# Attention stage of a hybrid decoder trunk: casts of weight pieces moved to GpSimd, four result splits made one, query projections taken in five passes

## The chip, the core and the metric

The kernel runs on one core of a Trainium2 chip. The metric is the device time of one execution in microseconds. Before the change it is 1218.23 us, the median of three runs (1217.66 to 1218.72). The five engines of the core are named as in the profile: PE (TensorE, matrix products; PEld is its loading of stationary operands), DVE (VectorE), ACT (ScalarE), POOL (GpSimd) and SP (SyncE, which here only issues DMAs).

## The reference

The input is one sequence of 512 rows with 1024 features in float32. Layer one is a gated recurrence with a SwiGLU feed-forward block. Then keys and values are computed once. Layer two is attention with another SwiGLU block. Only the attention matters here:

```python
def dilated_attention_mixer(h, w_q, q_norm, w_o, k, v, cos, sin):
    q = (h @ w_q).reshape(B, S, N_GROUPS, Q_HEADS, HEAD_DIM)      # 3 groups, 8 heads, 128
    q = apply_partial_rope(rms_norm(q, q_norm[:, None, :]), cos, sin)
    ...
    for g, (window, dilation) in enumerate(DILATION_GROUPS):      # (128,1), (512,4), (2048,16)
        o, l = dilated_window_attention(q[:, :, g], k[:, :, g], v[:, :, g], window, dilation)
    wts = softmax(stack(lses), axis=0)
    o = sum(wts[..., None] * stack(outs), axis=0)
    return o.reshape(B, S, 1024) @ w_o
```

There are two key/value heads, and each serves four query heads.

## The kernel before

**Exact products from two parts.** Every float32 operand of a large product is split into a high part in a shorter format (`fp32r`) and the low part that is left, and `mm3` (lines 146 to 148) or lines 703 to 705 issue three products for one: high by high, high by low, low by high. A weight comes in pieces of 128 x 1024 numbers, 512 KB each.

**The weight stream** is the class `Stream`. A piece `i` is loaded by SP into a tile `wr` (line 85, two buffers). Line 100 casts it to its high part `wh`, always on ACT. The low part `wl` is made in one of two ways. For most pieces DVE subtracts (line 107). For pieces marked "dma", which are the query weights `w_q`, the output weights `w_o` and seven pieces of the first stage, ACT writes minus one times the piece in the short format into `wl` (line 103), and a DMA issued by POOL adds the piece from memory once more onto it (line 104). `wh` and `wl` have three buffers each. `ws.get(i)` hands out piece `i` and prepares pieces up to `i+2` (`ws.asp = 2` in this stage), so the tiles of piece `i` become free when PE is done with piece `i-3`.

**Query projections** (`project_q`, `project`). For one key/value head a pass computes, for one group `g`, four tiles of 128 rows by 512 columns (four heads) from four pieces. A pass over all four row tiles takes 16 steps, four to a piece; one step is six products of 512 columns. A pass over two row tiles takes 8 steps, two to a piece, and loads the four pieces for itself. When a row tile is finished, `collect` scales and squares it, `rotate` applies the rotation, `normed` the factors, and `turn` transposes it on PE (line 781) and copies it out on ACT (line 783, `qt`). `at(n, ...)` holds such follow-up work for n ticks of a counter that each step advances.

**The units.** Attention proper is 32 units: two key/value heads, four row tiles, four phases. A unit has `scores` (PE products with keys, two DVE instructions for mask and minimum, the exponential on ACT at line 854, the reciprocal on DVE, the division on POOL at line 856); three units later `turned` (PE transposes at line 868, high part `ph` on ACT and low part `pl` on DVE by `halve`, lines 228 and 229); four units later, for odd phases, `values`. After the fourth phase of a row tile `values` writes the results of four heads: for the first three row tiles of the first head they are copied to `o_t`, for the other five row tiles they are split at once into `xh` and `xl`, head by head, by four calls of `halve`.

**Filling.** Head 0's projections run before the units. A table `plan` spreads the work for head 1 and the first half of the output projection (`out_half`, generator `o0`) between units: each row of it has a generator, a number of steps and the first and last unit between which they are dealt out. `q1` has 48 steps: a full pass for each of groups 0 and 1, and two half passes for group 2. Its first 11 steps (`START_Q`) run ahead of the units.

**The order on an engine** is fixed when the program is built. The code is recorded as written, a scheduler then places instructions by priority, and splits of weight pieces are recorded with high priority. On the chip each engine runs its list in that order, waiting by semaphores.

Of the kernel before, what the change touches and what calls it, by code (L numbers as in the profile page):

```python
# [69 lines left out]
class Stream:  # L70


    def __init__(self, tc, nc, pool, pieces, ahead_load, ahead_split):
        self.tc, self.nc, self.pool, self.pieces = tc, nc, pool, pieces
        self.al, self.asp = ahead_load, ahead_split
        self.raw, self.parts = {}, {}
        self.nl = self.ns = self.cut = 0
        self.hold = {}

    def _load(self, i):  # L80
# [10 lines left out]
    def _split(self, i):  # L91
        nc = self.nc
        r, w = self.raw.pop(i)
        hi = self.pool.tile([128, 1024], F32R, name=f"wh{i}", tag="wh")
        lo = self.pool.tile([128, 1024], F32R, name=f"wl{i}", tag="wl")
        self.parts[i] = (hi, lo)

        def do(c):
            with self.tc.high_priority():
                nc.scalar.copy(hi[:, c], r[:, c])  # L100
                kind = self.pieces[i][1]
                if kind == "dma":
                    nc.scalar.mul(lo[:, c], r[:, c], -1.0)  # L103
                    nc.gpsimd.dma_start(lo[:, c], self.pieces[i][0][:, c], accum_op=ALU.add)
                else:
                    eng = nc.gpsimd if kind == "pool" else nc.vector
                    a = eng.tensor_tensor(lo[:, c], r[:, c], hi[:, c].bitcast(F32), ALU.subtract)  # L107
# [32 lines left out]
def trunk(tc, A, out):  # L140
# [27 lines left out]

    p_f1 = ffn_pieces("f1_in", "f1_out")
    p_kv = add_pieces([A["w_kv"][i] for i in range(12)])  # L170
    p_q = add_pieces([A["w_q"][i] for i in (*range(24), *range(20, 24))], "dma")
    p_o = add_pieces([A["w_o"][i] for i in range(8)], "dma")
    p_f2 = ffn_pieces("f2_in", "f2_out")

    with tc.tile_pool(name="keep", bufs=1) as kp, tc.tile_pool(name="wts", bufs=3) as wp, \
# [104 lines left out]
        with tc.tile_pool(name="lru", bufs=2) as lp, \  # L280
# [243 lines left out]
STATS = 5  # L524
N_PR = 4
LAG_T, LAG_V = 3, 4
START_Q = 11


def rotary(tc, A, rp, tp):  # L530
# [67 lines left out]
def attention(tc, A, ap, ws, env):  # L598
# [170 lines left out]
    qt = {}  # L769

    def project_q(kv):
        for g in range(3):

            for j, tiles in enumerate((range(2), range(2, 4)) if kv and g == 2 else (range(4),)):
                def done_q(t, ps, g=g, st={}, tiles=tiles):
                    collect(ps, 4, t - tiles[0], len(tiles), st, t, 3 + g)
                    if t == tiles[-1]:
                        def turn(j, rows):
                            pt = bank("PT")
                            for i in range(4):  # L780
                                PE.transpose(pt[:, 128 * i:128 * i + 128], rows[:, 128 * i:128 * i + 128], ident)  # L781
                            q = ap.tile([128, 4, 4, 32], F32, name="qt", bufs=12)
                            S.copy(q, pt.rearrange("q (h p i) -> q p h i", h=4, p=4))
                            qt[j, kv, g] = q
                            if not kv and not j:
                                query_part(0, 0, g)

                        normed(st, 4, 0, turn, 8 if len(tiles) > 2 else 5, tiles)

                yield from project(p_q + 12 * kv + 4 * g + 4 * j, xh, xl, done_q, tiles)  # L790

    def first(fn):

# [81 lines left out]
    def values(kv, n, p):  # L875
# [21 lines left out]
        if kv == 0 and n < 3:  # L897
            S.copy(o_t[:, :, ns].rearrange("q h (p i) -> q h p i", p=4), src)
        else:
            for i in range(4):  # L900
# [136 lines left out]
```

## Time and profile before

| what | value |
|---|---|
| three timed runs, median (range) | 1218.23 us (1217.66 to 1218.72) |
| the profiled execution: its own time; its span | 1220.25 us; 1218.3 us |
| PE busy, share of span | 1204.8 us, 99% |
| DVE, ACT, POOL busy | 658.2, 514.4, 157.2 us |
| DMA, mean | 113 GB/s |
| mean granted clock of PE | 0.998 |

The sum of a prediction is made against the 1220.25 us of the profiled execution; 1.95 us of it lie outside the span. The stages can be told by their lines: recurrence to about 160 us, first feed-forward to about 520 us, keys and values to about 585 us, head 0's query projections and the first steps of head 1's to about 673 us, the units with their filling to about 828 us, then the rest of the output projection and the second feed-forward.

In the groups of the profile a row names line, engine and operation, output and inputs, count, busy time and mean duration, then the idle time of the engine ahead of these instructions and what ended it. In the tables by windows each engine has its busy time in the window and the number of instructions, then the granted clock (1.00 is full), the mean busy share of the 16 DMA engines and their GB/s.

### The profile page before, as it was taken

How to read it: one execution, taken by the hardware profiler on the slowest of the kernel's cores; microseconds unless marked ns; L12 is line 12 of the kernel's file. 1: busy time of each engine (PE TensorE's matmuls, PEld its weight loads, DVE VectorE, ACT ScalarE, POOL GpSimd, SP SyncE). 2: the span in 40 equal slices, each digit the busy share in tenths (PEclk: the TensorE clock that was granted, in tenths of full speed). 3: DMA queues.
4: the chain of work that ended last, by engine and by line, in shares of the span. 5: the costliest groups of instructions: out<-in, count | busy, mean ns of one | idle time of the engine just before them, and what ended most of it. 6: DMA issues, size and time to landing. Idle time of an engine off the chain costs nothing.

```text
span 1218.3 us, 14685 instructions
## 1 busy us (share of the span) xinstructions
PE 1204.8 (99%) x5627; PEld 995.6 (82%) x5627; DVE 658.2 (54%) x1237; ACT 514.4 (42%) x758; POOL 157.2 (13%) x159
## 2 busy tenths in 40 slices
PE   8999999999999999999999999999999999999998
PEld 6778888888888888888888887898888888888887
DVE  7787674454544333377564567765554455542221
ACT  6795433233232222265555667655423232222110
POOL 0100001011110000010411243341011011110000
PEclk9999999999999999999999999999999999999999
DMA  6643333323233333333988666335223323233341
GB/s 237 145 104 104 104 106 104 104 87 103 87 103 100 89 100 96 100 96 94 227 179 178 135 153 151 79 70 137 88 87 104 103 88 104 87 100 112 113 115 44
DMA packets 40757, 137.62 MB, mean 113 GB/s; under 512 B 5104, under 2 KB 5744, under 8 KB 40688
## 3 DMA queue, kind: packets, MB, share of 16 engines
q1 hardware_dynamic: 32976, 112.00, 28.9%
q0 software_dynamic: 6704, 23.60, 11.0%
q10 hardware_dynamic: 1008, 1.09, 0.3%
q8 instruction: 44, 0.72, 0.2%
q14 instruction: 25, 0.20, 0.0%
HBM read 133.53 MB, written 2.10 MB: 111 GB/s over the span
## 4 chain that ended last, share of the span: by engine, by line
PE 94%; DVE 3%; ACT 2%; DMA 1%; issue 0%; SPq 0%; DVEq 0%; ACTq 0%
PE ps L147 25%; PE ps L148 25%; PE ps L146 25%; PE ps L703 5%; PE ps L705 5%; PE ps L704 5%; DMA wr<-in_w_in 1%; PE ps L781 1%; PE ps L868 1%; PE ps L387 1%; PE ps L386 1%; ACT wh L100 0%; DVE sqc L640 0%; PE ps L245 0%; DVE pl L229 0%
## 5 line engine op out<-in xcount | busy, mean ns | idle before, releaser
L100 ACT CAST wh<-wr 128x1024 fp32r<-128x1024 f32 (+3 forms) x212 | 215.4, 1017 | 480.9 <-PE ps L147 444.3
L146 PE MATMUL ps<-xh,wh 128*128 128x512 f32 x896 | 352.7, 394 | 0.6 <-ACT xh L223 0.6
L148 PE MATMUL ps<-xh,wl 128*128 128x512 f32 x896 | 349.5, 390 | 0.4 <-DVE wl L107 0.4
L147 PE MATMUL ps<-xl,wh 128*128 128x512 f32 x896 | 349.4, 390 | 0.1
L107 DVE TENSOR_TENSOR wl<-wr,wh 128x1024 fp32r<-128x1024 f32 (+2 forms) x169 | 240.9, 1426 | 148.3 <-ACT wh L100 148.2
L146 PEld LDWEIGHTS ps<-xh,wh 128*128 128x128 f32 x896 | 168.3, 188 | 37.5 <-ACT xh L223 1.5
L147 PEld LDWEIGHTS ps<-xl,wh 128*128 128x128 f32 x896 | 168.5, 188 | 36.1 <-issue 1.7
L148 PEld LDWEIGHTS ps<-xh,wl 128*128 128x128 f32 x896 | 168.4, 188 | 35.8 <-DVE wl L107 0.8
L146 PE MATMUL ps<-gh,wh 128*128 128x512 f32 x352 | 137.0, 389 | 0.0
L148 PE MATMUL ps<-gh,wl 128*128 128x512 f32 x352 | 136.9, 389 | 0.0
L147 PE MATMUL ps<-gl,wh 128*128 128x512 f32 x352 | 136.9, 389 | 0.0
L491 POOL TENSOR_TENSOR u<-u,g 128x512 f32<-128x512 f32 x44 | 58.8, 1336 | 503.4 <-ACT wh L100 354.2
L490 DVE TENSOR_TENSOR u<-ps,rb 128x512 f32<-128x512 f32 x44 | 30.4, 691 | 135.9 <-PE ps L148 135.9
L703 PE MATMUL ps<-wh,xh 128*128 128x512 f32 x224 | 91.5, 408 | 0.4 <-DVE sqc L640 0.4
L705 PE MATMUL ps<-wh,xl 128*128 128x512 f32 x224 | 88.0, 393 | 0.0
L704 PE MATMUL ps<-wl,xh 128*128 128x512 f32 x224 | 87.5, 391 | 0.0
L148 PEld LDWEIGHTS ps<-gh,wl 128*128 128x128 f32 x352 | 66.1, 188 | 13.8
L147 PEld LDWEIGHTS ps<-gl,wh 128*128 128x128 f32 x352 | 66.1, 188 | 13.8
L146 PEld LDWEIGHTS ps<-gh,wh 128*128 128x128 f32 x352 | 66.1, 188 | 13.5
L488 DVE TENSOR_TENSOR g<-ps,rb 128x512 f32<-128x512 f32 x44 | 30.4, 691 | 63.7 <-PE ps L148 63.6
L103 ACT ACTIVATE wl<-wr 128x1024 fp32r<-128x1024 f32 x43 | 45.5, 1058 | 21.7 <-PE ps L704 20.8
L856 POOL TENSOR_SCALAR pr<-pr,den 128x512 f32<-128x512 f32 (+2 forms) x32 | 44.8, 1406 | 63.5 <-DVE den L855 60.5
(213 smaller groups left out, 1439.8 us busy)
## 6 DMA issues: line engine op xcount, KB each, us to landing
wr<-in_f_in SPq DMA_DIRECT2D x88, 512.0 KB, 3.5
wr<-in_f_out SPq DMA_DIRECT2D x32, 512.0 KB, 3.5
wr<-in_w_q SPq DMA_DIRECT2D x28, 512.0 KB, 6.5
wl<-in_w_q POOLq DMA_DIRECT2D x28, 512.0 KB, 7.3
wr<-in_w_in SPq DMA_DIRECT2D x14, 512.0 KB, 3.7
wr<-in_f_out SPq DMA_DIRECT2D x16, 384.0 KB, 3.2
wr<-in_w_kv SPq DMA_DIRECT2D x12, 512.0 KB, 3.5
wr<-in_a_out SPq DMA_DIRECT2D x8, 512.0 KB, 3.5
```

Of the source, the lines that this page charges most:

```text
L100: nc.scalar.copy(hi[:, c], r[:, c])
L103: nc.scalar.mul(lo[:, c], r[:, c], -1.0)
L107: a = eng.tensor_tensor(lo[:, c], r[:, c], hi[:, c].bitcast(F32), ALU.subtract)
L146: PE.matmul(ps, wh, xh, start=first, stop=False)
L147: PE.matmul(ps, wh, xl, start=False, stop=False)
L148: PE.matmul(ps, wl, xh, start=False, stop=last)
L488: V.tensor_tensor(g, pair[0], rb, ALU.mult)
L491: G.tensor_tensor(u, u, g, ALU.mult)
L703: PE.matmul(ps[t], xh[k][:, r], wh[:, c], start=k == 0, stop=False)
L704: PE.matmul(ps[t], xh[k][:, r], wl[:, c], start=False, stop=False)
L705: PE.matmul(ps[t], xl[k][:, r], wh[:, c], start=False, stop=k == 7)
L856: G.tensor_scalar(pr[:, :width], pr[:, :width], den, None, ALU.mult)
```

## The change

Five things are edited.

- `Stream` gets a field `cast`. While the units run (from the start of the units until the first half of the output projection is drained) line 100 uses POOL's copy in place of ACT's. Outside it stays on ACT.
- Line 103 negates the high part `wh` (already cast) and no longer the loaded piece `wr`. The value is the same; the instruction now has to come after the cast.
- Head 1's projections take five passes in place of four: group 0 over four row tiles, then groups 1 and 2 over the first two row tiles, then groups 1 and 2 over the last two. The steps stay 48. The pieces of group 1 are loaded and split twice now, as those of group 2 were before: 32 pieces of `w_q` in place of 28. `START_Q` is 10, the plan deals out 22, 12, 4 and 16 steps where it had 29, 4, 4 and 16, and with other bounds. The transposes of a finished half pass come 8 ticks later (7 for the last two row tiles), where it was 5.
- The eight tiles `xh` become eight views of one tile, likewise `xl`, and the results of four heads are split by one call of `halve` over 128 x 512 numbers in place of four over 128 x 128.
- In the first stage a callback of `in_block` runs after the sixth block of columns in place of the third.

```diff
         def do(c):
             with self.tc.high_priority():
-                nc.scalar.copy(hi[:, c], r[:, c])
+                (self.cast or nc.scalar.copy)(hi[:, c], r[:, c])
                 kind = self.pieces[i][1]
                 if kind == "dma":
-                    nc.scalar.mul(lo[:, c], r[:, c], -1.0)
+                    nc.scalar.mul(lo[:, c], hi[:, c].bitcast(F32), -1.0)
                     nc.gpsimd.dma_start(lo[:, c], self.pieces[i][0][:, c], accum_op=ALU.add)
...
-    p_q = add_pieces([A["w_q"][i] for i in (*range(24), *range(20, 24))], "dma")
+    p_q = add_pieces([A["w_q"][i] for i in (*range(24), *range(16, 24))], "dma")
...
-        xh = [kp.tile([128, T], F32R, name=f"xh{k}") for k in range(KB)]
-        xl = [kp.tile([128, T], F32R, name=f"xl{k}") for k in range(KB)]
+        xhs, xls = (kp.tile([128, KB * T], F32R, name=n).rearrange("q (k t) -> q k t", k=KB) for n in ("xh", "xl"))
+        xh, xl = ([x[:, k] for k in range(KB)] for x in (xhs, xls))
...
-                    if k == 2 and between:
+                    if k == 5 and between:
...
-START_Q = 11
+START_Q = 10
...
-            for j, tiles in enumerate((range(2), range(2, 4)) if kv and g == 2 else (range(4),)):
+        early, late, every = range(2), range(2, 4), range(4)
+        passes = [(0, every), (1, early), (2, early), (1, late), (2, late)] if kv else [(g, every) for g in range(3)]
+        for j, (g, tiles) in enumerate(passes):
...
-                        normed(st, 4, 0, turn, 8 if len(tiles) > 2 else 5, tiles)
+                    normed(st, 4, 0, turn, 7 if tiles is late else 8, tiles)
...
-            for i in range(4):
-                halve(src[:, i], xh[4 * kv + i][:, ns].rearrange("q (p i) -> q p i", p=4),
-                      xl[4 * kv + i][:, ns].rearrange("q (p i) -> q p i", p=4))
+            halve(src, *(x[:, 4 * kv:4 * kv + 4, ns].rearrange("q h (p i) -> q h p i", p=4)
+                         for x in (env["xhs"], env["xls"])))
...
-    plan = [(q1, 40 - START_Q, 0, 12), (q1, 4, 12, 15), (q1, 4, 15, 18.5), (o0, 16, 20, 37)]
+    plan = [(q1, 32 - START_Q, 0, 12.5), (q1, 12, 12.5, 17), (q1, 4, 17, 18.5), (o0, 16, 20, 36)]
     given, stage = [0] * len(plan), {}
+    ws.cast = G.tensor_copy
...
     drain(o0)
     ws.asp = 1
+    ws.cast = None
```

How the lists of two engines move is shown at three places. Line numbers of the changed kernel are one or two higher than before: its lines 101, 104, 105, 229, 640, 785, 856 and 858 are the old 100, 103, 104, 228, 639, 783, 854 and 856.

ACT near the end of head 0's query projections, before:

```order
L639 ACTIVATE ps<-ps 128x512
L103 ACTIVATE wl_4928<-wr_4925 128x1024
L100 CAST wh_4927<-wr_4925 128x1024
L783 COPY qt<-ps 128x512
L228 CAST qh<-qt 128x512
L103 ACTIVATE wl_4977<-wr_4974 128x1024
L100 CAST wh_4976<-wr_4974 128x1024
```

and now:

```order
L101 CAST wh_4913<-wr_4911 128x1024
L104 ACTIVATE wl_4914<-wh_4913 128x1024
L785 COPY qt<-ps 128x512
L229 CAST qh<-qt 128x512
L101 CAST wh_4962<-wr_4960 128x1024
L785 COPY qt<-ps 128x512
L104 ACTIVATE wl_4963<-wh_4962 128x1024
```

Where the negation stood ahead of the cast of the same piece, it stands behind it now, so the DMA that POOL issues on the negation is behind both.

POOL in the middle of the units, before (`pr` is the division of a unit, line 856):

```order
L104 DMA wl_5640<-in_w_q 128x1024
L856 TENSOR_SCALAR pr<-pr,den 128x384
L104 DMA wl_5790<-in_w_q 128x1024
L856 TENSOR_SCALAR pr<-pr,den 128x512
L104 DMA wl_5840<-in_w_q 128x1024
```

and now:

```order
L858 TENSOR_SCALAR pr<-pr,den 128x384
L105 DMA wl_5694<-in_w_q 128x1024
L858 TENSOR_SCALAR pr<-pr,den 128x512
L101 CAST wh_5736<-wr_5734 128x1024
L105 DMA wl_5737<-in_w_q 128x1024
L101 CAST wh_5804<-wr_5802 128x1024
L858 TENSOR_SCALAR pr<-pr,den 128x512
L105 DMA wl_5805<-in_w_q 128x1024
```

A cast joins each DMA on POOL's list, ahead of it, and a division may stand between the two. There are 21 such casts on POOL; ACT's list loses 17.

ACT where the results of the last row tile of head 0 are split (the first of the five split places), before:

```order
L854 ACTIVATE pr,den<-pr,mn 128x256
L228 CAST xh_72<-ps 128x128
L228 CAST ph<-ps 128x2x128
L228 CAST xh_73<-ps 128x128
L228 CAST qh<-qt 128x512 x2
L228 CAST ph<-ps 128x2x128
L228 CAST xh_74<-ps 128x128
```

and now:

```order
L104 ACTIVATE wl_6536<-wh_6535 128x1024
L229 CAST xh<-ps 128x4x128
L229 CAST ph<-ps 128x2x128
L229 CAST qh<-qt 128x512 x2
L229 CAST ph<-ps 128x2x128
L856 ACTIVATE pr,den<-pr,mn 128x256
```

The second, third and fourth head's casts stood between the `ph` and `qh` of later units; now one cast stands ahead of all of them.

More of the change, by code (lines that the diff above doesn't have):

```diff
@@ L77, in __init__ @@
         self.nl = self.ns = self.cut = 0
+        self.cast = None
         self.hold = {}
@@ L771, in project_q, with done_q, turn @@
     def project_q(kv):
-        for g in range(3):
-            for j, tiles in enumerate((range(2), range(2, 4)) if kv and g == 2 else (range(4),)):
[L775 to L779, printed above, removed]
-                            for i in range(4):
[L781 to L786, printed above, removed]
-                        normed(st, 4, 0, turn, 8 if len(tiles) > 2 else 5, tiles)
-                yield from project(p_q + 12 * kv + 4 * g + 4 * j, xh, xl, done_q, tiles)
+        early, late, every = range(2), range(2, 4), range(4)
+        passes = [(0, every), (1, early), (2, early), (1, late), (2, late)] if kv else [(g, every) for g in range(3)]
+        for j, (g, tiles) in enumerate(passes):
+            def done_q(t, ps, g=g, st={}, tiles=tiles):
+                collect(ps, 4, t - tiles[0], len(tiles), st, t, 3 + g)
+                if t == tiles[-1]:
+                    def turn(j, rows):
+                        pt = bank("PT")
+                        for i in range(4):
+                            PE.transpose(pt[:, 128 * i:128 * i + 128], rows[:, 128 * i:128 * i + 128], ident)
+                        q = ap.tile([128, 4, 4, 32], F32, name="qt", bufs=12)
+                        S.copy(q, pt.rearrange("q (h p i) -> q p h i", h=4, p=4))
+                        qt[j, kv, g] = q
+                        if not kv and not j:
+                            query_part(0, 0, g)
+                    normed(st, 4, 0, turn, 7 if tiles is late else 8, tiles)
+            yield from project(p_q + 12 * kv + 4 * j, xh, xl, done_q, tiles)
     def first(fn):
@@ L899, in values @@
         else:
-            for i in range(4):
-                halve(src[:, i], xh[4 * kv + i][:, ns].rearrange("q (p i) -> q p i", p=4),
-                      xl[4 * kv + i][:, ns].rearrange("q (p i) -> q p i", p=4))
+            halve(src, *(x[:, 4 * kv:4 * kv + 4, ns].rearrange("q h (p i) -> q h p i", p=4)
+                         for x in (env["xhs"], env["xls"])))
     def attend():
```

## The prediction

> **What bounds the kernel now.** First the page's busy times, then the table by windows. The rows are 600 to 670 us (head 0's query projections), three stretches of the units, a stretch of the second feed-forward block, and two short windows in the middle of the units.
>
> ```profile
> PE 1204.8 (99%) x5627; PEld 995.6 (82%) x5627; DVE 658.2 (54%) x1237; ACT 514.4 (42%) x758; POOL 157.2 (13%) x159
> ...
> 600.00:670.00 70.00, 70.00 (x334) 57.87 (x333) 38.62 (x119) 39.70 (x55) 10.98 (x13) 1.00 0.84 188
> 675.00:730.00 55.00, 54.58 (x322) 47.15 (x322) 38.30 (x139) 35.93 (x65) 20.27 (x19) 1.00 0.63 136
> 730.00:785.00 55.00, 49.54 (x329) 43.46 (x327) 39.88 (x132) 39.49 (x78) 20.21 (x17) 0.97 0.59 133
> 785.00:825.00 40.00, 39.71 (x283) 36.25 (x283) 25.24 (x85) 24.27 (x56) 18.96 (x14) 1.00 0.25 57
> 900.00:925.00 25.00, 25.00 (x112) 20.70 (x111) 13.76 (x12) 7.13 (x9) 3.58 (x3) 1.00 0.28 87
> ...
> 770.00:780.00 10.00, 8.31 (x56) 7.79 (x55) 9.32 (x40) 6.04 (x17) 4.31 (x5) 0.85 0.46 105
> 780.00:790.00 10.00, 9.91 (x70) 8.73 (x70) 5.56 (x20) 5.57 (x16) 3.30 (x3) 0.98 0.01 2
> ```
>
> PE is the bound, and outside the units it never stops: in 900 to 925 us it is busy throughout, at 25 / 112 = 0.223 us per product of 512 columns. The change leaves PE's products as they are, so it can only gain what PE loses in the units. The table gives that: 55 - 49.54 = 5.5 us of idle PE in 730 to 785, 0.4 ahead of it and 0.3 behind it, together 6.2 us. To this comes the clock: 0.15 x 10 + 0.02 x 10 = 1.7 us lost in 770 to 790. So at most 7.9 us, 0.65% of the whole, can be won; a loss has no such limit.
>
> The second view is the list of waits, for PE between 670 and 830 us (what waited, for whom; total, times, longest).
>
> ```profile
> PE ps L146 <- ACT ph L228: 1.7, 1, 1.7
> PE ps L146 <- DVE mn L849: 1.5, 2, 1.0
> PE ps L781 <- DVE kn L669: 0.8, 1, 0.8
> PE ps L781 <- ACT qt L783: 0.7, 1, 0.7
> PE ps L146 <- ACT qh L228: 0.6, 1, 0.6
> PE ps L703 <- DVE sqc L640: 0.4, 1, 0.4
> PE ps L147 <- DVE pl L229: 0.3, 1, 0.3
> ```
>
> That is 6.0 us: 3.0 on ACT, 3.0 on DVE, and nothing on a weight piece. The last point decides the case, since the change makes weights scarcer. The third view, the timeline, shows the longest wait (ACT's rows, then PE's).
>
> ```profile
> 772.22 0.27 ACT L228 CAST xh<-ps 128x128 fp32r<-128x128 f32 x1
> 772.51 0.37 ACT L228 CAST ph<-ps 128x256 fp32r<-128x256 f32 x1
> 774.63 0.27 ACT L228 CAST xh<-ps 128x128 fp32r<-128x128 f32 x1 [1.74 <-DVE xl L229]
> 775.83 0.37 ACT L228 CAST ph<-ps 128x256 fp32r<-128x256 f32 x1
> ...
> 776.25 0.38 PE L146 MATMUL ps<-ph,vh 128*128 128x256 f32 x1 [1.69 <-ACT ph L228]
> ```
>
> The split of the results goes head by head between ACT and DVE. The second head's cast stands at the front of ACT's list and waits 1.74 us for DVE's `xl`; DVE is 93% busy in that window. The `ph` that PE needs stands behind it. PE sits 1.69 us, and from there the clock is low.
>
> The Trainium skill (TensorE: Matmul & The Clock Gate, "Why this matters for your kernels") advises against idle gaps of over about 3 us between products, since such a gap brings the half clock. Here the longest gap is 1.7 us and the clock still fell. By that rule the fall has another cause than this gap, and removing the gap would win 1.7 us; by the rows, where the low clock follows the gap at once, 3.4.
>
> **The change part by part.** The prices come from these groups (670 to 830 us, the POOL cast from the whole span):
>
> ```profile
> L856 POOL TENSOR_SCALAR pr<-pr,den 128x512 f32<-128x512 f32 (+2 forms) x32 | 44.8, 1406 | 63.5 <-DVE den L855 60.5 <-PE ps L147 3.0
> L103 ACT ACTIVATE wl<-wr 128x1024 fp32r<-128x1024 f32 x17 | 18.0, 1059 | 4.8 <-PE ps L704 4.0 <-DMA wr<-in_w_q 0.8
> L100 ACT CAST wh<-wr 128x1024 fp32r<-128x1024 f32 x17 | 17.6, 1038 | 0.0
> L229 DVE TENSOR_TENSOR xl<-ps,xh 128x128 fp32r<-128x128 f32 x19 | 5.5, 287 | 5.8 <-ACT xh L228 5.8
> L228 ACT CAST xh<-ps 128x128 fp32r<-128x128 f32 x20 | 5.3, 263 | 10.0 <-DVE xl L229 6.1 <-PE ps L148 3.9
> L104 POOL DMA_DIRECT2D wl<-in_w_q x11 | 9.8, 888 | 24.1 <-ACT wl L103 24.1
> ...
> 519.82 4.51 POOL L722 CAST xp<-xl 128x512 fp32r<-128x512 f32 x8
> ```
>
> *Results in one pass.* Twenty casts and twenty subtractions become five of each, and the hand-over between ACT and DVE happens once in a place, not four times. With one cast ahead of it `ph` no longer stands behind DVE. I take away the 1.7 us wait and the 1.7 us of clock behind it: **-3.4 us**. Bounds: -1.7 if the clock falls anyway, -3.4.
>
> *Casts off ACT.* ACT loses 17 casts of 1.04 us and gains four negations of 1.06 us, 13.4 us less in the units. PE's waits on `qt` (0.7) and `qh` (0.6) lie where ACT had casts of weights and of `o_t` in a row: **-1.3 us**, bounds 0 and -1.3.
>
> *Later transposes.* PE waited 0.8 us for `kn`, which DVE scales just ahead of a transpose; the transposes of half passes now come 7 or 8 ticks behind and not 5: **-0.8 us**, bounds 0 and -0.8. Of the 1.5 us on `mn` (DVE, the minimum that frees the scores' bank) I take half, since DVE is hardly relieved (15 short subtractions fewer) while the work of groups 1 and 2 no longer bunches: **-0.7 us**, bounds +0.5 and -1.5. The remaining 0.7 us stay.
>
> *POOL's new load.* The eight casts of 512 columns took 4.51 us, so one of 1024 takes about 2 x 0.564 = 1.13 us. Twenty-one casts are 24 us, four more DMA issues 3.6 us; beside 45 us of divisions and 15 us of issues POOL comes to 87 of 160 us. It is no bound. What a cast holds up on POOL is a division, needed by PE three units later; a unit takes some 2.5 us of PE without filling (160 us, less 53 steps of 6 x 0.223 us, less 7.7 us lost, over 32), so the cover is over 7 us. The same rows of the timeline show what two engines cost each other:
>
> ```profile
> 277.28 2.33 DVE L107 TENSOR_TENSOR wl<-wr,wh 128x1024 fp32r<-128x1024 f32 x1 [0.21 <-ACT wh L100]
> 282.72 1.23 DVE L107 TENSOR_TENSOR wl<-wr,wh 128x1024 fp32r<-128x1024 f32 x1 [0.21 <-ACT wh L100]
> ...
> 759.22 1.56 POOL L856 TENSOR_SCALAR pr<-pr,den 128x512 f32<-128x512 f32 x1 [1.17 <-DVE den L855]
> ...
> 760.02 1.28 DVE L229 TENSOR_TENSOR ql<-qt,qh 128x512 fp32r<-128x512 f32 x2
> ```
>
> In the feed-forward block every other subtraction on DVE takes 2.33 and not 1.23 us; the `ql` subtractions, also of two tiles, keep 0.64 us each beside a POOL division. A cast is nearer to the division (one input tensor), so I put **+0.2 us**, bounds 0 and +1.5.
>
> The Trainium skill (GPSIMD Engine Reference, "Key points") says that POOL shares its interfaces to SBUF with DVE and collides with DVE instructions that have two inputs there. The 760.02 row does not bear that out for POOL work with one input; by the rule a cast could hold such an instruction up by the 1.1 us between the first two rows.
>
> *The wait that may come in.* A piece's low part is now cast, negation, DMA; it was negation, DMA. The order lists show it at the end of head 0's projections too. There the pieces are used 5.4 us apart or more, and the 1 us that the DMA starts later I cost at nothing; the cover is that two pieces take 10.7 us of PE, against the chain's 9.7 (below), and it is thin: bound +1. In the units it is another matter. The chain for one piece, before:
>
> ```profile
> 716.51 1.06 ACT L103 ACTIVATE wl<-wr 128x1024 fp32r<-128x1024 f32 x1
> ...
> 717.87 0.90 POOL L104 DMA_DIRECT2D wl<-in_w_q  x1 [3.03 <-ACT wl L103]
> ...
> DMA to landing us min/median/max: 6.2/7.3/9.1
> ...
> q0 software_dynamic: 1940, 6.77, 56.3%
> q1 hardware_dynamic: 1728, 6.29, 27.1%
> ...
> wl<-in_w_q POOLq DMA_DIRECT2D x13, 512.0 KB, 7.0
> wr<-in_w_q SPq DMA_DIRECT2D x12, 512.0 KB, 6.4
> ```
>
> From the negation's start to landing it took 1.36 + 7.3 = 8.7 us; it can start when PE is done with the piece three back. The POOL cast makes that 8.7 + 1.1 + some 0.1 for one more hand-over = 9.9 us (8.8 to 11.7 with the fastest and slowest landing). PE's demand: in the last 16 steps of `q1` (units 12.5 to 18.5) a half-pass piece goes with 0.75 unit, 0.75 x 2.5 + 12 x 0.223 = 4.6 us, for eight pieces in a row; the eight before it come every 1.14 units, 5.5 us. Before the change only four pieces came that fast (29 steps in 12 units: 4.8 us), then 6.4 and 7.1 us. Two pieces at 4.6 us give 9.2 us, plus what unit work follows a piece's last product, against a chain of 9.9. A delay shifts what comes after, so it is paid about every second piece: four times 0.7 is 2.8 us; some unit work counts for it: **+2.0 us**. Bounds: 0 with the fastest landing, and +10 with the slowest (11.7 - 9.2 = 2.5, four times).
>
> The last four rows (600 to 670 us) give the DMA engines' own bound: 0.563 x 70 / 13 = 3.0 us for an adding DMA, 0.271 x 70 / 12 = 1.6 us for a load, 4.6 us a piece at full share. The demand is just that.
>
> *First stage.* The callback moves two short normalisation pieces; PE does not wait on them there for more than 0.9 us in all, and they stay in PE's order: nothing, ±0.3.
>
> The sum: -3.4 - 1.3 - 0.8 - 0.7 + 0.2 + 2.0 = **-4.0 us**. The profiled execution becomes 1216.2, its span 1214.3; it ran 2.0 us above the median of 1218.23, so the median becomes **1214.2 us**.
>
> **The rivals.**
>
> *Weights become the bound (slower).* For the high demand: no stall on weights is in the list, landings had 9.1 us at worst, and the DMA share was 0.84 at 5.6 us a piece (12.5 pieces in 70 us). Mechanism: in units 12.5 to 18.5 each pair of pieces waits for its adding DMA, and the loads, released by POOL's cast, queue on the same engines. At the slow end +10 in place of +2.0 gives +4.0: **1222 us**. It decides once a piece takes over 5.4 us there (8 x 0.8 = 6.4 against the 6.2 won). Against it: pieces prepared ahead in the slower stretch.
>
> *The waits stay on DVE.* DVE is at 93% in 770 to 780. If `mn` and `kn` wait as before and the casts hold DVE up by 1.5 us, it is -3.4 - 1.3 + 2.0 + 1.5 = -1.2: **1217 us**.
>
> *All of it goes.* No wait on weights, and the whole 7.9 us is won: **1210.3 us**. For it: scheduling placed all 17 pieces without a stall before.
>
> *One tile in place of eight.* If products of the output projection had to wait for splits of other heads, each of four row tiles would cost PE up to 0.6 + 0.7 us, +5: 1219 us. The projections read `xh` of head 0, the splits write head 1, so I give it little.
>
> **How the numbers follow.** The forecast has 46%, all of it won 15%, the waits on DVE 21%, weights 15%, the one tile 3%. A change within 0.2% (2.4 us, about what a measurement of this kernel can tell) ends at 1215.8 and 1220.7. Faster: 42 of the forecast's 46, all 15, 3 of the second: 0.60. Same: 4, 17, 2 of the weights' and the 3 of the one tile: 0.26. Slower: the rest, 0.14. The likeliest case's own range is 1211.5 to 1216.5; to leave out no more than 2 in 10 the range goes from 1209.8, just past the full gain, to 1219.5.
>
> **What would show it.** In the changed profile the wait of PE on `ph` L228 near the split of results is gone and the granted clock is 1.00 in all windows of the units; PE's waits on ACT fall under 0.5 us. If weights bind, a wait of PE on `wl` appears in units 12 to 18, the DMA share there is over 0.9, and landings are over 8 us. If DVE binds, `mn` and `kn` stay in the list with 2 us or more. POOL's casts should take 1.1 to 1.4 us. Wrong would be: PE's idle time in the units over 6 us again, or idle PE under 2 us with the time unchanged, since then the loss was not in what PE waited for.

## The result and the profile after

The change makes the kernel slower: 1228.89 us (median of four, 1227.37 to 1233.36) beside 1218.02 us (1217.66 to 1218.72) for the kernel before. The ratio is 1.0095, 95% interval 1.0073 to 1.0117; a second set of runs gave 1.0094 (1.0081 to 1.0107). The forecast was 1214.2 us, and the range ended at 1219.5.

The profiled execution took 1227.37 us with a span of 1225.6. It is the fastest of the four, so its trace shows 7.1 us of the loss (against the 1220.25 us of the profile before). First the busy times of the page, then five of the eight windows of the units (PE, PEld, DVE, ACT and POOL busy, granted clock, DMA share, GB/s), then what PE waited for between 670 and 830 us.

```profile
PE 1209.0 (99%) x5627; PEld 996.9 (81%) x5627; DVE 665.7 (54%) x1231; ACT 502.6 (41%) x730; POOL 184.7 (15%) x184
```

```profile
670.00:690.00 20.00, 18.98 (x114) 16.06 (x113) 13.54 (x47) 10.42 (x21) 9.28 (x10) 1.00 0.61 131
690.00:710.00 20.00, 17.67 (x109) 14.76 (x109) 15.00 (x48) 12.87 (x25) 10.41 (x10) 1.00 0.76 173
...
750.00:770.00 20.00, 18.87 (x105) 15.89 (x103) 16.78 (x46) 12.77 (x24) 9.76 (x9) 0.91 0.81 180
770.00:790.00 20.00, 17.79 (x116) 15.87 (x115) 14.71 (x56) 10.40 (x24) 9.21 (x9) 0.91 0.58 129
...
810.00:830.00 20.00, 18.89 (x130) 16.75 (x130) 11.28 (x33) 9.65 (x19) 10.72 (x8) 1.00 0.28 60
```

```profile
PE ps L148 <- DVE pl L230: 2.4, 3, 1.8
PE ps L149 <- DVE ql L230: 2.2, 5, 1.0
PE ps L783 <- DVE kn L670: 2.1, 2, 1.8
PE ps L147 <- DVE mn L851: 1.1, 2, 0.8
PE ps L147 <- ACT ph L229: 0.7, 2, 0.4
PE ps L148 <- DVE vl L230: 0.3, 1, 0.3
```

DVE has six instructions fewer than before and is busy 7.5 us longer: some of its instructions took longer. PE's waits on ACT fell from 3.0 to 0.7 us, nearly as hoped, but its waits on DVE rose from 3.0 to 8.1. No wait on a weight piece is in the list. The clock is low in two windows, where it was in one. A second profile of the same kernel had a span of 1229.7 us at a mean clock of 0.994 (here 0.997): part of the scatter is how often the clock fell.

At the place where the results are split, the wait of 1.7 us on `ph` is gone and another has its place (PE's rows, then DVE's).

```profile
779.26 0.39 PE L147 MATMUL ps<-ph,vh 128*128 128x256 f32 x1 [0.28 <-ACT ph L229]
781.48 0.39 PE L148 MATMUL ps<-pl,vh 128*128 128x256 f32 x1 [1.83 <-DVE pl L230]
```

```profile
779.06 0.17 DVE L220 SCALAR_TENSOR_TENSOR qr4y<-qr4a,qr4y 128x8 f32<-128x8 f32 x1
779.26 0.69 DVE L670 TENSOR_TENSOR kn<-kn,qr4y 128x512 f32<-128x512 f32 x1
779.87 0.42 DVE L230 TENSOR_TENSOR pl<-ps,ph 128x256 fp32r<-128x256 f32 x1
780.21 0.68 DVE L230 TENSOR_TENSOR xl<-ps,xh 128x512 fp32r<-128x512 f32 x1
...
781.01 0.42 DVE L230 TENSOR_TENSOR pl<-ps,ph 128x256 fp32r<-128x256 f32 x1
```

`ph` comes in time now, but the `pl` that is needed next stands on DVE behind a scaling of `kn`, another `pl`, the one large `xl` and a mask. PE waits 1.83 us, as long as before.

### The profile page after: what moved, and what is told of

The parts are those of the page before. It is cut to its first block, busy times and chain, and to the rows that moved or that the text cites. A ratio compares the mean times of both kernels' runs of the same rounds, so it can differ in the third digit from the quotient of the medians.

```text
span 1225.6 us, 14703 instructions
## 1 busy us (share of the span) xinstructions
PE 1209.0 (99%) x5627; PEld 996.9 (81%) x5627; DVE 665.7 (54%) x1231; ACT 502.6 (41%) x730; POOL 184.7 (15%) x184
## 4 chain that ended last, share of the span: by engine, by line
PE 91%; DVE 4%; ACT 2%; DMA 1%; issue 1%; POOL 1%; ACTq 0%; DVEq 0%; POOLq 0%
PE ps L148 25%; PE ps L149 25%; PE ps L147 25%; PE ps L704 5%; PE ps L705 5%; PE ps L706 5%; PE ps L783 1%; DMA wr<-in_w_in 1%; PE ps L387 1%; PE ps L388 1%; DMA wl<-in_w_q 1%; PE ps L870 1%; ACT wl L104 0%; ACT pr L856 0%; POOL wh L101 0%
## 5 line engine op out<-in xcount | busy, mean ns | idle before, releaser
L101 ACT CAST wh<-wr 128x1024 fp32r<-128x1024 f32 (+3 forms) x195 | 198.1, 1016 | 495.3 <-PE ps L148 440.5
L104 ACT ACTIVATE wl<-wh 128x1024 fp32r<-128x1024 f32 x47 | 49.7, 1058 | 11.3 <-POOL wh L101 10.6
L229 ACT CAST gh<-u 128x512 fp32r<-128x512 f32 x44 | 27.4, 622 | 62.1 <-POOL u L492 62.1
```

The source lines that it names most:

```text
L101: (self.cast or nc.scalar.copy)(hi[:, c], r[:, c])
L104: nc.scalar.mul(lo[:, c], hi[:, c].bitcast(F32), -1.0)
```

## The experiments

All times are device microseconds; the ratio is to the kernel before on the same chip. The rows in the order of the sections:

| kernel | median us | ratio (95%) |
|---|---|---|
| c100: casts on POOL, negative from the high part | 1226.38 | 1.0066 (1.0051 to 1.0081) |
| m010: one split of the results | 1219.56 | 1.0008 (0.9998 to 1.0017) |
| p001: five passes, plan, later transposes | 1223.42 | 1.0040 (1.0025 to 1.0055) |
| mp011: the change without its casts, its negative and the first-stage callback | 1222.19 | 1.0033 (1.0021 to 1.0044) |
| b36: before, output projection to unit 36 | 1223.26 | 1.0034 (1.0022 to 1.0047) |
| p37: p001, output projection to unit 37 | 1218.69 | 0.9996 (0.9986 to 1.0006) |
| start19: p37, output projection from unit 19 | 1219.19 | 1.0008 (0.9995 to 1.0020) |
| extra: before, POOL also copies each raw piece | 1227.00 | 1.0062 (1.0045 to 1.0078) |
| craw: c100, negative from the raw piece | 1222.12 | 1.0029 (1.0019 to 1.0038) |
| hol: extra, ACT's negative behind the copy | 1225.28 | 1.0055 (1.0041 to 1.0068) |
| craw4: craw, each cast in four | 1222.06 | 1.0025 (1.0015 to 1.0035) |
| araw37c4: araw37 (below), each cast in four | 1218.06 | 0.9997 (0.9985 to 1.0008) |
| a37: the change, output projection to unit 37 | 1229.17 | 1.0076 (1.0051 to 1.0102) |
| a37b: the same, once more | 1228.48 | 1.0079 (1.0066 to 1.0093) |
| after2: the change, once more | 1230.12 | 1.0094 (1.0081 to 1.0107) |
| araw: the change, negative from the raw piece | 1225.12 | 1.0059 (1.0045 to 1.0073) |
| araw37: both of these | 1219.64 | 1.0011 (1.0000 to 1.0021) |
| mpk37: araw37, casts on ACT | 1218.13 | 0.9993 (0.9982 to 1.0005) |

### The parts alone

The working theory (A) came from the trace after: a cast on POOL holds up DVE's instructions that read two tensors of SBUF. The rival (B) puts the loss on the five passes and their plan.

The edit of c100 (the core of it) in the kernel before:

```diff
-                nc.scalar.copy(hi[:, c], r[:, c])
+                (self.cast or nc.scalar.copy)(hi[:, c], r[:, c])
...
-                    nc.scalar.mul(lo[:, c], r[:, c], -1.0)
+                    nc.scalar.mul(lo[:, c], hi[:, c].bitcast(F32), -1.0)
...
+    ws.cast = G.tensor_copy
```

> The kernel before with one part of the change alone: during the units the high parts of the weights are cast on POOL (and the negative is taken from the high part); five passes and the single split of results are left out. Theory A (a POOL cast of 1.09 us holds up every VectorE instruction that reads two tensors of SBUF until it is over, and TensorE then waits for VectorE): the small wins on ACT (up to 1.3 us) are outweighed, 1220 to 1224 us, and TensorE's waits on DVE in the units rise from 3.0 us to 5 or more. Theory B (the five passes and the new plan cost the time, the casts are harmless): 1216.5 to 1218, waits on DVE stay near 3.

Measured 1.0066, some 8.0 us: a loss as A said, and larger. PE's waits on DVE in the units came to 6.4 us.

m010 has the joint tile for `xh` and `xl` and the one split:

```diff
-            for i in range(4):
-                halve(src[:, i], xh[4 * kv + i][:, ns]..., xl[4 * kv + i][:, ns]...)
+            halve(src, *(x[:, 4 * kv:4 * kv + 4, ns]... for x in (env["xhs"], env["xls"])))
```

> The kernel before with the single split of four heads' results alone. If the 1.7 us wait for ph and the half clock behind it were due to the four separate splits, as predicted: 1214.5 to 1215.5 us. If VectorE's factor chain stands in the way of pl there in any case (theory A's reading of the changed kernel, where TensorE waited 1.83 us for pl at that place): 1217 to 1219, the wait moved from ph to pl.

Measured 1.0008. PE's wait between 770 and 835 us in it, the only one there:

```profile
PE ps L147 <- DVE pl L229: 2.0, 1, 2.0
```

So the split wins nothing by itself: the wait goes from `ph` to `pl` with no cast on POOL involved, as the second reading had it.

p001 has the new `project_q`, the new table and the later transposes; mp011 has the split beside it.

```diff
-    plan = [(q1, 40 - START_Q, 0, 12), (q1, 4, 12, 15), (q1, 4, 15, 18.5), (o0, 16, 20, 37)]
+    plan = [(q1, 32 - START_Q, 0, 12.5), (q1, 12, 12.5, 17), (q1, 4, 17, 18.5), (o0, 16, 20, 36)]
```

> The kernel before with the five passes, the plan and the later transposes alone; casts stay on ACT, results are split in four. Theory A: 1215 to 1219 (kn and mn waits move a little, no POOL hold added). Theory B: 1224 to 1229, most of the loss is here.

> The changed kernel with the casts back on ACT (single split, five passes and plan kept). Theory A: the loss is gone, 1214 to 1219 us, VectorE's busy time falls from 665.7 to about 658 to 660. Theory B: 1224 to 1229.

1.0040 and 1.0033, between the two ranges: neither theory alone holds. Casts and plan each cost several microseconds without the other.

### What in the passes costs: one number of the plan

p001 waited for `ph` in units 23 to 31, where the passes had long ended. There only the last row of the plan differs, 36 for 37.

```diff
-    plan = [..., (q1, 4, 17, 18.5), (o0, 16, 20, 36)]
+    plan = [..., (q1, 4, 17, 18.5), (o0, 16, 20, 37)]
```

> p001 (five passes alone) with the 16 pieces of output projection spread over units 20 to 37, as in the kernel before, in place of 20 to 36. Theory E (the shorter plan moves the filling work from behind the scores to ahead of the turning, so that the results of units 23 to 31 follow the scores at once and wait for ph): TensorE's waits for ph fall from 4.6 us to about 1.7, 1217 to 1220 us. Rival (the passes themselves cost it): 1222 to 1225 as p001.

> The kernel before with the 16 pieces of output projection over units 20 to 36 in place of 37, nothing else. Theory E: the waits for ph appear here too, 1220.5 to 1223 us. Rival (the passes): 1218 to 1219, as before.

Both came out as theory E had it: b36, one number away from the kernel before, comes to 1.0034; p37 costs nothing that can be measured. The windows from 790 to 830 us, of before, b36 and p37 in turn:

```profile
790.00:830.00 40.00, 39.71 (x278) 36.07 (x277) 24.05 (x76) 22.17 (x49) 16.47 (x12) 1.00 0.36 80
```

```profile
790.00:830.00 40.00, 36.67 (x251) 32.62 (x250) 21.56 (x70) 20.27 (x44) 16.47 (x12) 1.00 0.30 68
```

```profile
790.00:830.00 40.00, 39.99 (x273) 36.11 (x273) 23.17 (x72) 21.42 (x48) 16.46 (x12) 1.00 0.35 80
```

PE is idle for 0.3, 3.3 and 0.0 us. The order shows why. In the kernel before, six products of the output projection stand between the last score product and the results (804.41 to 805.94); in b36 they stand ahead of the transposes (`ident,pr`), and the results follow the scores at once. Before, then b36:

```profile
804.41 0.28 PE L148 MATMUL ps<-kh,kl 128*128 128x128 f32 x1
804.52 0.45 PE L146 MATMUL ps<-xh,wh 128*128 128x512 f32 x1
...
805.94 0.28 PE L146 MATMUL ps<-ph,vh 128*128 128x256 f32 x1
```

```profile
804.95 0.60 PE L868 MATMUL ps<-ident,pr 128*128 128x128 f32 x4
...
806.25 0.28 PE L148 MATMUL ps<-kh,kl 128*128 128x128 f32 x1
807.57 0.38 PE L146 MATMUL ps<-ph,vh 128*128 128x256 f32 x1 [1.04 <-ACT ph L228]
```

ACT needs the transposes and then its own time for `ph`; the filling work that covered this was moved. The passes and the later transposes themselves did their part: in p37 the waits for `kn`, `mn` and `qt` fell from 3.0 us together to 0.7. Its longest waits of PE between 670 and 830 us:

```profile
PE ps L146 <- ACT ph L228: 2.4, 1, 2.4
PE ps L704 <- DMA wl<-in_w_q: 0.6, 1, 0.6
PE ps L782 <- DVE kn L669: 0.4, 1, 0.4
PE ps L146 <- DVE mn L850: 0.3, 1, 0.3
```

One wait of 2.4 us is left, for `ph` where the results are split, and a short one for a weight piece, `wl`, has come in. start19 tried to cover the first:

```diff
-    plan = [..., (o0, 16, 20, 37)]
+    plan = [..., (o0, 16, 19, 37)]
```

> The five passes with the casts on ACT, results split in four and the output projection over units 19 to 37. In p37 the last wait above 1 us was TensorE's for ph, 2.4 us, where scores were followed by the results of unit 15 at once; with the start at 19 six matmuls of a projection (1.6 us) lie between the turning and those results. If the half clock of 3.4 us follows that wait, both go: 1214 to 1216.5. If the wait stays: 1217 to 1219, as p37.

1.0008: the wait went from 2.4 to 1.3 us, but to another unit (803 us), and the clock fell all the same. Nothing was won.

### What in the casts costs

extra leaves ACT's work as it was and only lets POOL copy each raw piece onto itself.

```diff
                     nc.scalar.mul(lo[:, c], r[:, c], -1.0)
+                    if self.extra:
+                        nc.gpsimd.tensor_copy(r[:, c], r[:, c])
```

> The kernel before, casts left on ACT, with one more POOL instruction for each weight piece in the units: the raw piece (128x1024) is copied onto itself once ACT has read it. Nothing that the units compute needs it, ACT never waits for it, so only POOL's and VectorE's shared way to SBUF and the reload of the raw buffer can feel it. Theory A (a POOL copy of 1.1 us holds VectorE's two-input instructions): VectorE's busy time rises from 658 by 4 to 7 us, the wait of TensorE for mn and kn grows, 1221 to 1226 us. Theory D (c100's loss comes from ACT, which stands still while its negative waits for POOL's cast): 1217.5 to 1219, as before.

1.0062, as A said and a little above its range; DVE was busy for 664.7 us, 6.5 more than before, and PE waited for no weight piece in the units. Its longest wait of PE in the units, with the row of POOL, the row of DVE and the row of PE:

```profile
684.52 1.35 POOL L106 COPY wr<-wr 128x1024 f32<-128x1024 f32 x1
```

```profile
682.84 0.29 DVE L652 TENSOR_TENSOR ra<-kn,cc 128x128 f32<-128x128 f32 x1
...
684.32 1.70 DVE L652 TENSOR_TENSOR ra<-kn,cc 128x128 f32<-128x128 f32 x1
```

```profile
687.68 0.50 PE L706 MATMUL ps<-wh,xh 128*128 128x512 f32 x1 [2.61 <-DVE sqc L643]
```

The same product `ra` takes 0.29 us alone and 1.70 us beside the copy; it began 0.2 us ahead of the copy and ended 0.15 us behind it. An instruction with a single input in SBUF was held as well; it takes 0.17 us otherwise (POOL, then DVE):

```profile
725.05 1.18 POOL L106 COPY wr<-wr 128x1024 f32<-128x1024 f32 x1
```

```profile
725.10 1.17 DVE L213 TENSOR_SCALAR qr4y<-sqc 128x16 int32<-128x16 int32 x1
```

In the changed kernel the factor chain is caught in the same way (POOL, then DVE, then the wait of PE for the `kn` that the chain scales):

```profile
693.24 1.26 POOL L101 CAST wh<-wr 128x1024 fp32r<-128x1024 f32 x1
```

```profile
693.13 0.18 DVE L218 TENSOR_TENSOR qr4a<-qr4a,qr4y 128x16 f32<-128x16 f32 x1
693.34 1.20 DVE L219 SCALAR_TENSOR_TENSOR qr4a<-qr4a 128x16 f32<-128x16 f32 x1
694.58 0.18 DVE L220 SCALAR_TENSOR_TENSOR qr4y<-qr4a,qr4y 128x16 f32<-128x16 f32 x1
```

```profile
695.74 0.66 PE L783 MATMUL ps<-ident,kn 128*128 128x128 f32 x4 [1.77 <-DVE kn L670]
```

An instruction on 16 columns takes 1.20 us, and it ends just after the cast has ended (694.54 and 694.50 us). Each DVE instruction between 670 and 835 us can be compared with the usual time of its own kind (the median of its line, tiles and shape, differences over 0.1 us counted). The trace of before has 1.1 us too much in 5 cases, all beside divisions; that after has 8.9 us in 17: 7.0 us beside casts (11 cases), 1.9 beside divisions (6).

craw takes the other new link out. In c100 ACT's negative reads what POOL casts, so ACT waits for it.

```diff
-                    nc.scalar.mul(lo[:, c], hi[:, c].bitcast(F32), -1.0)
+                    nc.scalar.mul(lo[:, c], r[:, c], -1.0)
```

> The kernel before with the casts on POOL during the units, but ACT's negative is still taken from the raw piece, so that ACT no longer waits for POOL's cast (10.0 us of such waits on ACT in c100). Theory A: no better than c100, 1224 to 1228 us. Theory D: most of c100's loss is gone, 1217 to 1220.

1.0029, between the two readings: more than half of c100's loss is gone. DVE's time lost beside casts fell too, from 5.5 us to 4.2, so part of this may be holds. But in the kernel araw, further below, the same edit won 4.3 us while as much was lost beside casts as in the change (7.7 and 7.0 us), so the wait has a price of its own. It can be followed in c100 (rows of POOL, ACT, DVE):

```profile
730.01 1.84 POOL L857 TENSOR_SCALAR pr<-pr,den 128x512 f32<-128x512 f32 x1 [2.52 <-PE ps L149]
731.82 1.03 POOL L101 CAST wh<-wr 128x1024 fp32r<-128x1024 f32 x1
```

```profile
732.88 1.06 ACT L104 ACTIVATE wl<-wh 128x1024 fp32r<-128x1024 f32 x1 [3.11 <-POOL wh L101]
733.85 0.71 ACT L855 ACTIVATE pr<-pr,mn 128x512 f32<-128x512 f32 x1
```

```profile
734.68 0.16 DVE L856 RECIPROCAL den<-den 128x1 f32<-128x1 f32 x1 [2.92 <-ACT pr L855]
```

The cast stands behind a division on POOL, the negative stands on ACT for 3.11 us, the exponential stands behind the negative, and DVE, also in order, waits 2.92 us for the exponential. In craw the same wait was 0.94 us. How it reaches PE is not shown step by step: PE's longest wait for `mn` in c100 comes eight microseconds later, behind a `ql` that a cast held as well (1.53 us, 0.69 in craw).

```profile
740.79 1.53 DVE L230 TENSOR_TENSOR ql<-qt,qh 128x512 fp32r<-128x512 f32 x1
```

```profile
742.87 0.35 PE L147 MATMUL ps<-kh,qh 128*128 128x256 f32 x1 [1.82 <-DVE mn L850]
```

ACT waited for casts for this long between 670 and 835 us (c100, then the changed kernel):

```profile
ACT wl L104 <- POOL wh L101: 10.0, 11, 3.1
```

```profile
ACT wl L104 <- POOL wh L101: 10.6, 8, 2.4
```

hol was to price ACT's wait apart from the casts: the copy of extra, placed ahead of the negative.

```diff
+                    if self.extra:
+                        nc.gpsimd.tensor_copy(r[:, c], r[:, c])
                     nc.scalar.mul(lo[:, c], r[:, c], -1.0)
```

> The kernel before with the casts on ACT and POOL's copy of the raw piece onto itself as in the kernel named extra, but placed ahead of ACT's negative, which so waits for it. Same load on POOL, same reads and writes; only ACT stands still meanwhile. If ACT's wait costs by itself: 3 to 9 us above extra's 1227. If ACT's wait is harmless and the copy alone costs: 1225 to 1229.

It did not add to extra: 1.0055, although ACT waited 13.9 us for the copies. In hol only 2.8 us of DVE's time were lost beside copies, in 4 cases; in extra 6.1 us in 8. The move changed both at once, so hol doesn't settle the price of ACT's wait; it shows that such a wait need not cost. That this depends on what stands behind it is likely, but not shown.

craw4 asks how POOL holds DVE, and araw37c4 puts the same to use:

```diff
-                (self.cast or nc.scalar.copy)(hi[:, c], r[:, c])
+                if self.cast:
+                    for d in range(c.start, c.stop, 256):
+                        self.cast(hi[:, d:d + 256], r[:, d:d + 256])
+                else:
+                    nc.scalar.copy(hi[:, c], r[:, c])
```

> craw (casts on POOL, negative from the raw piece) with each cast in four instructions of 128x256. If one POOL instruction holds a VectorE instruction until it is over, the longest hold falls from about 1.0 us to about 0.3, VectorE's extra time beside casts from 4.2 us to 2 or less, 1219 to 1221 us. If the two share the way in proportion to what POOL moves: extra time stays near 4 us, 1222 to 1223.

> araw37 with each cast in four in the same way, the best form of the change that keeps the casts on POOL. By the first reading 1217.5 to 1219 us (araw37 was 1219.64); by the second 1219 to 1221.

The holds became shorter, most of them 0.2 us, as "until it is over" has it, but more: 13 with 3.3 us in all, for 6 with 4.2 in craw. The longest was still 0.9 us, for an instruction beside several parts in a row. POOL pays as well: the four parts of a piece keep it busy for 29.3 / 17 = 1.7 us and not 1.1 (craw4, then craw).

```profile
L103 POOL CAST wh<-wr 128x256 fp32r<-128x256 f32 x68 | 29.3, 498 | 24.2 <-PE ps L710 16.9 <-PE ps L152 5.7 <-POOL pr L861 1.7
```

```profile
L101 POOL CAST wh<-wr 128x1024 fp32r<-128x1024 f32 x17 | 19.3, 1136 | 25.9 <-PE ps L706 18.3 <-PE ps L148 5.6 <-POOL pr L857 1.9
```

The time stayed: 1.0025 for 1.0029, and 0.9997 for araw37's 1.0011, whose intervals overlap. By the time alone craw4 (1222.06 us) falls in the range of the second reading and araw37c4 (1218.06 us) in that of the first, so the time does not decide between them.

### The change taken apart

Starting from the changed kernel: a37 takes the plan's end back, araw37 the negative as well, mpk37 the casts as well.

```diff
-    plan = [..., (o0, 16, 20, 36)]
+    plan = [..., (o0, 16, 20, 37)]
...
-                    nc.scalar.mul(lo[:, c], hi[:, c].bitcast(F32), -1.0)
+                    nc.scalar.mul(lo[:, c], r[:, c], -1.0)
...
-    ws.cast = G.tensor_copy
```

> First step of taking the changed kernel apart: the changed kernel with the output projection over units 20 to 37, nothing else. If the plan costs here what it costs in the kernel before (4.8 us): 1223 to 1225.5. If the casts cover or replace it: 1227 to 1229, as the changed kernel.

> Second step: the same, and ACT's negative taken from the raw piece again, so that ACT doesn't wait for POOL's cast. If that wait costs here what it costs without the other parts (c100 less craw, 4.3 us): 1219 to 1222, and the 10.6 us that ACT waited for the cast are gone. If only VectorE's hold matters: as a37, 1223 to 1225.5.

> Third step: the casts back on ACT too; what is left of the change is the single split of results, the five passes, the later transposes and the later place of the turning in the first stage. If VectorE's hold by POOL's casts is the third part (craw, 3.7 us): 1216.5 to 1219.5. If something in these parts costs as well: 1220 or more.

The first step won nothing clear, as its second reading had it, the second won 9.5 us where 4.3 were expected, and the third came out within its first range. So the plan (a37b) and the change itself (after2) were run again beside a kernel with only the negative put back (araw):

> The changed kernel with one line put back: ACT's negative is taken from the raw piece and no longer waits for POOL's cast; casts stay on POOL, the plan stays at 20 to 36. If that wait is the main part of the loss (a37 less araw37: 9.5 us): 1219 to 1222. If the plan costs 4 to 5 us beside it, as it does in the kernel before: 1222 to 1225. If it was a37 that ran by chance at a low clock: 1225 or more.

> a37 once more, in more runs and beside the changed kernel on the same chip: the output projection over units 20 to 37. If the plan costs nothing while ACT waits for the casts: within 1.5 us of the changed kernel. If it costs 4 to 5 us: that much below it.

> The changed kernel itself, once more, as the measure for the two others of this call: 1227 to 1230.

araw came to 1225.12 us, at the border of its second and third reading; a37b to 1.6 us less than the change, close to its first reading; the change to 1230.12 us.

Building up from mpk37 (0.9993), with one thousandth as 1.22 us: casts on POOL +2.2 us (araw37, 1.0011; the two intervals overlap), the plan to 36 +5.9 (araw, 1.0059), the negative from the cast +4.3 (after2, 1.0094). In the other order the negative comes first with +8.3 (a37b, 1.0079), and the plan adds 1.8, again with intervals that overlap. The three together make the 12 us between mpk37 and the change, but the shares of plan and negative depend on which is there already; each of them costs 4 to 5 us in the kernel before (b36; c100 less craw). What else the change does, mpk37, is no difference that can be measured.

No kernel is faster than the kernel before by more than can be measured. The lowest medians, 1218.06 (araw37c4), 1218.13 (mpk37) and 1218.69 us (p37), cannot be told from it.

## Why the prediction was wrong, step by step

The sum priced what the change takes away. What the change adds was priced at +0.2 us for POOL's load, and at nothing for ACT's new wait on POOL and for the earlier end of the plan. Measured one at a time these three cost 2.2 to 3.5, 4.3 to 8.3 and 1.8 to 5.9 us, depending on what else is there. The largest gain of the sum, -3.4 us for the single split, did not come, because another wait stood right behind the one taken away.

- **What bounds the kernel.** Right in the place: the loss is in the units, and the sentence that a loss has no such limit as the 7.9 us of gain is what happened. The windows add up to 9.2 us of idle PE in 670 to 830 us, for 6.2 before. Idle PE and low clock are not all of it: PE's busy time rose by 4.2 us (1204.8 to 1209.0) for the same 5627 products, and 6.8 us at half clock where it was 3.4 explain 1.7 of them. Where the other 2.5 us lie is not shown; a product ahead of a wait counts as busy to its end (0.39 us at 779.26), and this may be part of it.
- **Results in one pass, -3.4.** Wrong. The step took away the wait for `ph` without asking what was late next. `pl` was: 1.8 us (2.0 in m010), and the clock fell behind it as before, so neither of the two times 1.7 us was won. m010 gives +1.0 us, with 0 inside its interval.
- **Casts off ACT, -1.3.** The waits for `qt` and `qh` did go. But the edit of the negative was read only as a link in a weight's chain. It also puts ACT behind POOL, and ACT is in order: the exponential, `ph` and `qh` stand behind the negative. Nothing in the sum answers for it. It costs 4.3 us (c100 against craw by the medians; after2 against araw by the ratios) to 8.3 (a37b against araw37).
- **Later transposes, -0.8 and -0.7.** Right where they can be seen: with casts on ACT and the old end of the plan (p37) the waits for `kn` and `mn` fell from 2.3 to 0.7 us together, 0.1 more than forecast. In the changed kernel `kn` was late again (2.1 us), behind held instructions of the factor chain and a held scaling.
- **POOL's new load, +0.2.** Wrong by its size and by its rule. A cast was put beside the division on the strength of one row of two `ql` subtractions that were not held; the division had ended at 760.78 us, so only the first of them ran wholly beside it. The same trace had five other instructions held beside divisions, by 1.1 us in all. Casts held DVE for 7.0 us and, less what ACT gained, cost 2.2 us (araw37 against mpk37) to 3.5 us (craw); the bound was 1.5.

  The trace after decides: of 30 DVE instructions other than accumulator reads and reciprocals that began during a cast, those with an operand in PSUM (17) lost nothing; of 13 with both operands in SBUF 11 were held, ten of them until 0.02 to 0.15 us past the cast's end, and the other two began in its last 0.06 us. Beside divisions it was different: of 28 instructions with both operands in SBUF that began during one, 22 lost at most 0.05 us and six lost 0.17 to 0.53 us.

  The Trainium skill (GPSIMD Engine Reference, "Key points"), which the prediction had set aside, is borne out for the casts. Its page SBUF — State Buffer ("SBUF: two separate sides") says more: the shared pair of ports is an exclusive lock for a whole instruction, against a POOL operation that reads SBUF; the rows of the casts agree, with 1.03 us more for an instruction of 0.17, those of the divisions do not.
- **Weights arriving later, +2.0, and the rival of 1222 us.** Did not happen in the changed kernel. No wait on `wl` is in the units of the profile after, the DMA share stays at 0.85 or less there, and the median landing fell from 7.3 to 6.4 us. One wait of 1.1 us for `wl` lies at 601 us, in head 0's projections; the second profile of the change has none, and m010, without any cast moved, has one of 1.4, so the new link is not needed for it. With the casts on ACT the five passes did bring short waits for `wl` in the units: 0.6 us in p37, 0.4 in mpk37, 1.0 in start19. The margin was thin, as the prediction said.
- **The end of the plan.** The prediction used the plan for the demand on weights alone. The row of the output projection, 36 for 37, had no term. It costs 4 to 5 us by itself (b36).
- **What would show it.** The prediction's own tests were good: the wait on `ph` went, yet the clock did not become 1.00; `kn` with 2.1 us is half of the sign it gave for DVE as the bound (`mn` has 1.1, while `pl` and `ql`, which it did not name, have over 2 each); and "over 6 us" of idle PE was named as what would prove it wrong. Of the rivals, the one with waits staying on DVE (1217 us) had the right place, but put 1.5 us where PE's waits on DVE rose by 5.1, and it still came out as a gain.

## What to carry to other kernels

Before an elementwise operation goes to POOL, look at which DVE instructions will run beside it: here those with two inputs in SBUF waited for the end of a cast of 128x1024, however small they were, while those that read PSUM did not; beside the divisions most ran on. When an instruction gets a new input, ask whose queue that input stands in, and what stands behind the waiting instruction on its own engine. And where filling work covers a latency, one step more or less in a table of due times can move it to the wrong side of the operation that it covers; compare the order at each place, not only the amounts.

## What the runs showed of the hardware

The low clock comes in stretches of 3.41 us or multiples of it. One such window of before, and two of the second profile of the change (start and end taken from the trace's clock records):

```profile
776.96:780.37 3.41, 3.41 (x14) 2.94 (x13) 2.74 (x11) 1.46 (x5) 2.38 (x2) 0.50 0.01 5
```

```profile
695.01:698.42 3.41, 3.41 (x13) 2.72 (x11) 2.32 (x8) 1.57 (x4) 1.04 (x2) 0.50 0.96 228
783.76:790.58 6.82, 6.38 (x24) 5.69 (x25) 3.63 (x15) 1.68 (x5) 3.02 (x2) 0.50 0.20 38
```

These three came with waits of PE of 1.7 to 1.8 us: two began 0.5 to 0.7 us after the wait had ended, the third 0.4 us before its end. So such a wait may cost another 1.7 us of clock for each 3.41 us. But it does not do so every time: the first profile of the change kept the full clock after its 1.77 us that ended at 695.7 us, where the second lost it, and lost it at 759.2 us behind three waits of 0.2 to 0.4 us. What brings the low clock stays open. Two executions of one kernel thus differ by several microseconds, and this limits how finely parts can be added up here.
